# Routing of a gathered token block dealt out differently: three heads sorted early, two pieces a turn

## The chip, the cores and the metric

The kernel runs on one core of a Trainium2 chip. The metric is device microseconds of one execution, lower is better: 1499.62 us is the median of three runs before (1498.49 to 1500.58). An execution with a profile was taken beside them.

## The reference

One encoder block on 512 tokens of 1024 channels: a gated half, an attention half, an output product, and then PEER, a retrieval over 128 x 128 single-neuron experts, which fills most of the time. For each block of 128 tokens PEER does this, 8 heads, 16 experts a head:

```python
q = (xb @ w_query).reshape(128, 8, 2, 128)
s = jnp.einsum('thpc,pkc->thpk', q, sub_keys)
s1, i1 = lax.top_k(s[:, :, 0], 16)
s2, i2 = lax.top_k(s[:, :, 1], 16)
cand = s1[..., :, None] + s2[..., None, :]
sc, ci = lax.top_k(cand.reshape(128, 8, 256), 16)
e = i1[ci // 16] * 128 + i2[ci % 16]
g = softmax(sc)
act = gelu(einsum('td,thkd->thk', xb, expert_u[e]))
out = einsum('thk,thkd->td', g * act, expert_v[e])
```

So each token has 16 lists of 128 scores (8 heads, two halves of the key), each of which is cut to its best 16; then each head chooses 16 among sums of the two lists, and the choices are decoded into expert numbers.

## The kernel before

The four blocks of 128 tokens go two ways. Three blocks are *dense*: all 16384 experts are computed for them, in 128 turns of 128 experts. The fourth block is *gathered*: for each of its tokens the 128 chosen expert rows are fetched by an indirect DMA (8 KB a row, 128 rows a fetch, one for each token), and VectorE does the dot product and the weighted sum.

**Query phase** (250 to 345 us of the trace). For each of 16 columns `c` (head `c // 2`, half `c % 2`), TensorE makes the queries of all four blocks, then the scores of 128 keys; ScalarE copies them to the tile `sc` (two buffers). VectorE sorts the three dense lists of the column with `top16` (maximum of 8, their indices, replace, maximum of 8, indices). The list of the gathered block is put away: `Q.dma_start(sd[:, c, :], sc[:, DB, :])` on line 732, a DMA of 64 KB on SyncE's queue to the tensor `sd` in HBM. TensorE meanwhile runs products of later turns, up to 31 of them (`AHEAD`). When VectorE has finished the dense routing, TensorE turns it (line 815).

**Turns** (from 562 us on, the loop over `e` in 0 to 127). Turn `e` has the same work each time:
- TensorE: 24 matmuls of a u product (line 200: 16 with `uhi`, 8 with `ulo`) of the experts that lie 36 turns ahead, then 18 matmuls of the v product of turn `e` (line 1007). From turn 92 on no u product is left, and only the 18 remain.
- ScalarE: casts `uhi`, `vhi` and `wahi` (lines 169 and 79), and the gelu `act` of the u product (line 759).
- VectorE: `wa` (line 992), `vlo` and `walo` (line 80), `ulo` (line 180): the rests that the casts leave. `uhi`, `ulo`, `vhi`, `vlo` have two buffers each.
- SyncE: the next 512 KB of `uraw`, the next 512 KB of `vraw`, every fourth turn 768 KB of `wt`.

Every engine runs its queue in the order in which the program was written, so a wait of VectorE holds up all that stands behind it.

**Routing of the gathered block.** `gather_routing` is a generator. It loads the 16 lists (`scg`, 1 MB) in turn 0, sorts the two lists of each of 8 heads, chooses for pairs of heads, and decodes four heads at a time (`decode`), with a softmax in between; it stops at each `yield`. In each turn, behind the turn's own VectorE work, three pieces are taken from it (line 1087). There are 26 pieces, so that it ends in turn 8 with the expert list `ei`; then the first four gathers are issued on GpSimd (line 953), and from turn 9 on `rate` dot products are put into each turn, a third of that in turns from 92 on. In a turn with dot products these stand ahead of `ulo` and `vlo` on VectorE. `rate` is 128 over the weighted number of turns left: 128 / (123 - 8 - 23.4) = 1.397 with an end in turn 8. In the tail it is 0.35 times that.

In `decode`, ScalarE's part is the copies into the one-hot tiles `oh` (line 676), between a part of VectorE that makes `rw`, `cl` and a part that compares and sums; the softmax has an exponential on ScalarE (line 700), which needs a load of its function table, and the next gelu another.

Names in the rows of the trace: `gs`, `gi` are the sorted values and indices of the gathered block (`late` in the code), `gtop`, `gci` the chosen ones, `uv` a gathered row.

## Time and profile before

| | |
|---|---|
| median of three runs | 1499.62 us |
| profiled execution | 1503.86 us |
| its span, first to last instruction | 1501.6 us |
| busy: TensorE matmuls, weight loads | 97%, 86% |
| busy: VectorE, ScalarE, GpSimd | 77%, 43%, 19% |
| granted TensorE clock, mean | 0.993 |
| DMA over the span | 359.31 MB, 239 GB/s |

The profiled execution is 4.2 us above the median; differences are taken within it and then set against the median. TensorE is busy nearly all the time, so that a share of the span says little here: what counts is where it stands still, and at which clock it runs right behind such a stop. The turns repeat to the hundredth of a microsecond where nothing disturbs them, so that a disturbed stretch can be measured as the excess over so many undisturbed turns.

### The profile page before, as it was taken

The numbers are of one execution on the slowest core, as the hardware profiler recorded it, in microseconds if no ns is written. First come the engines' busy times: TensorE is split into PE (matmuls) and PEld (weight loads), VectorE is DVE, ScalarE is ACT, GpSimd is POOL, SyncE is SP. The second block draws the span as 40 slices with busy tenths as digits, with TensorE's granted clock in tenths as the row PEclk, the third lists the DMA queues.
The fourth block names the chain that finished last, engine by engine and source line by source line (L and its number), as shares of the span: only waits on it lengthen the run. The fifth ranks groups of instructions, "written<-read, shape, count | busy, mean of one in ns | idle before, by whom it ended". The sixth has DMA issues, their size and how long they took to land.

```text
span 1501.6 us, 21590 instructions
## 1 busy us (share of the span) xinstructions
PE 1459.0 (97%) x7945; PEld 1296.2 (86%) x7945; DVE 1161.3 (77%) x2415; ACT 640.3 (43%) x1088; POOL 281.0 (19%) x222
## 2 busy tenths in 40 slices
PE   8999999998999999899999999999999999999997
PEld 6878988888888899789999999999999999987785
DVE  4745554799999958879888888888888888877765
ACT  5455753344555543343333333333333333324334
POOL 0140002445400000012222212222212221211002
PEclk9999999999999999999999999999999999999999
DMA  6331032332366775389999999899999999988764
GB/s 218 105 101 51 22 127 91 95 95 90 113 255 265 253 274 203 105 308 354 340 338 326 331 328 336 322 327 315 337 335 322 323 321 327 324 284 292 253 199 166
DMA packets 129641, 359.31 MB, mean 239 GB/s; under 512 B 9216, under 2 KB 60672, under 8 KB 113024
## 3 DMA queue, kind: packets, MB, share of 16 engines
q1 hardware_dynamic: 104048, 198.54, 40.3%
q0 software_dynamic: 18432, 134.23, 23.6%
q10 hardware_dynamic: 7056, 25.18, 4.2%
q8 instruction: 62, 1.02, 0.3%
q14 instruction: 43, 0.35, 0.1%
HBM read 327.50 MB, written 30.41 MB: 238 GB/s over the span
## 4 chain that ended last, share of the span: by engine, by line
PE 72%; DVE 13%; DMA 7%; ACT 3%; issue 3%; POOL 1%; ACTq 0%; SPq 0%; DVEq 0%; POOLq 0%
PE pu L200 31%; PE acc L1007 27%; PE acc L251 6%; DMA vraw<-in_uv_dram 4%; DVE ohb L846 3%; DVE ulo L180 2%; DVE oha L850 2%; DVE vlo L80 1%; DMA uraw<-in_uT_dram 1%; ACT vhi L79 1%; PE tr L729 1%; PE tr L433 1%; PE pu L251 1%; POOL ulo L180 1%; PE acc L446 1%
## 5 line engine op out<-in xcount | busy, mean ns | idle before, releaser
L200 PE MATMUL pu<-h2T,uhi 128*128 128x384 f32 (+2 forms) x2336 | 452.4, 343 | 4.9 <-ACT act L759 2.4
L200 PEld LDWEIGHTS pu<-h2T,uhi 128*128 128x128 f32 x2336 | 410.6, 189 | 21.3 <-ACT uhi L169 3.0
L953 POOL DMA_INDIRECT uv<-in_uv_dram,ei x128 | 168.3, 1315 | 844.0 <-DVE xlast L968 352.0
L80 DVE TENSOR_TENSOR vlo<-vraw,vhi 128x1024 fp32r<-128x1024 f32 x128 | 156.8, 1225 | 155.7 <-ACT vhi L79 155.7
L79 ACT CAST vhi<-vraw 128x1024 fp32r<-128x1024 f32 x128 | 134.6, 1051 | 287.2 <-issue 174.7
L200 PE MATMUL pu<-h2T,ulo 128*128 128x384 f32 (+2 forms) x1168 | 236.2, 342 | 7.4 <-DVE ulo L180 5.2
L1007 PE MATMUL acc<-vhi,wahi 128*128 128x512 f32 x768 | 239.4, 392 | 2.2 <-ACT wahi L79 2.2
L1007 PE MATMUL acc<-vlo,wahi 128*128 128x512 f32 x768 | 239.1, 392 | 0.4
L1007 PE MATMUL acc<-vhi,walo 128*128 128x512 f32 x768 | 238.2, 391 | 0.0
L200 PEld LDWEIGHTS pu<-h2T,ulo 128*128 128x128 f32 x1168 | 204.9, 189 | 13.8 <-DVE ulo L180 6.4
L169 ACT CAST uhi<-uraw 128x1024 fp32r<-128x1024 f32 x144 | 150.7, 1047 | 63.1 <-DMA uraw<-in_uT_dram 49.8
L1007 PEld LDWEIGHTS acc<-vlo,wahi 128*128 128x128 f32 x768 | 144.4, 189 | 33.9 <-DVE vlo L80 2.4
L1007 PEld LDWEIGHTS acc<-vhi,walo 128*128 128x128 f32 x768 | 144.2, 188 | 31.6 <-DVE walo L80 0.7
L968 DVE SCALAR_TENSOR_TENSOR xlast<-uv,dot,xlast 128x1024 f32<-128x1024 f32 x128 | 164.5, 1285 | 4.5
L1007 PEld LDWEIGHTS acc<-vhi,wahi 128*128 128x128 f32 x768 | 143.2, 188 | 27.3 <-ACT wahi L79 3.5
L959 DVE SCALAR_TENSOR_TENSOR uv<-uv,h 128x1024 f32<-128x1024 f32 x128 | 153.7, 1219 | 9.5 <-DMA uv<-in_uv_dram,ei 9.5
L180 DVE TENSOR_TENSOR ulo<-uraw,uhi 128x1024 fp32r<-128x1024 f32 x116 | 141.6, 1220 | 22.6 <-ACT uhi L169 22.3
L759 ACT ACTIVATE act<-pu 128x384 f32<-128x384 f32 x128 | 62.9, 491 | 220.6 <-PE pu L200 220.2
L180 POOL TENSOR_TENSOR ulo<-uraw,uhi 128x512 fp32r<-128x512 f32 x56 | 81.3, 1475 | 209.3 <-PE acc L251 106.3
L79 ACT CAST wahi<-wa 128x384 fp32r<-128x384 f32 x128 | 65.3, 510 | 41.2 <-DVE wa L992 41.2
L992 DVE TENSOR_TENSOR wa<-act,wt 128x384 f32<-128x384 f32 x128 | 70.6, 551 | 2.2 <-DMA wt<-wd 2.1
L80 DVE TENSOR_TENSOR walo<-wa,wahi 128x384 fp32r<-128x384 f32 x128 | 70.7, 553 | 0.6 <-ACT wahi L79 0.6
(250 smaller groups left out, 1475.7 us busy)
## 6 DMA issues: line engine op xcount, KB each, us to landing
uraw<-in_uT_dram SPq DMA_DIRECT2D x128, 512.0 KB, 6.1
vraw<-in_uv_dram SPq DMA_DIRECT2D x128, 512.0 KB, 5.6
wd<-wst ACTq DMA_DIRECT2D x48, 512.0 KB, 2.8
wt<-wd SPq DMA_DIRECT2D x32, 768.0 KB, 11.2
wraw<-in_w_in_dram SPq DMA_DIRECT2D x19, 512.0 KB, 3.7
uraw<-in_w_q_dram SPq DMA_DIRECT2D x16, 512.0 KB, 3.8
xT<-in_xT_dram SPq DMA_DIRECT2D x8, 256.0 KB, 3.7
xt<-in_x_dram SPq DMA_DIRECT2D x1, 2048.0 KB
```

The lines of the kernel that those rows point to most:

```text
L79: S.copy(hi, src)
L80: sub.tensor_tensor(lo, src, hi.bitcast(F32), op=ALU.subtract)
L169: S.copy(hi, raws[i])
L180: eng.tensor_tensor(lo[:, k, :], raws[i][:, k, :], hi[:, k, :].bitcast(F32), op=ALU.subtract)
L200: T.matmul(o, l[:, k, :], r[:, k, t0:n], start=(p == 0 and k == 0), stop=(p == 2 and k == KT - 1))
L251: T.matmul(out[b], l[:, b * 128:(b + 1) * 128], r[:, kk, :], start=(k == 0 and i == 0), stop=(k == KT - 1 and i == 2))
L759: S.activation(acts[e], o[:, :DT], AF.Gelu_apprx_tanh)
L953: G.indirect_dma_start(out=uvs[r].rearrange("p s d -> p (s d)"), out_offset=None, in_=A["uv"], in_offset=bass.IndirectOffsetOnAxis(ap=ei[: ...
L959: V.scalar_tensor_tensor(uv[:, 0, :], uv[:, 0, :], 1.0, h2, op0=ALU.mult, op1=ALU.mult, accum_out=d[:, 0:1])
L968: V.scalar_tensor_tensor(xlast, uv[:, 1, :], d[:, 1:2], xlast, op0=ALU.mult, op1=ALU.add)
L992: eng.tensor_tensor(wa.rearrange("p (c t) -> p c t", c=NWC), acts.pop(e).rearrange("p (c t) -> p c t", c=NWC), wts[e // WG][:, :, e % WG, ...
L1007: T.matmul(acc[b][n], l[:, c], r[:, n * 512:(n + 1) * 512], start=(e == 0 and i == 0), stop=(e == NK - 1 and i == 2))
```

## The change

Three edits, all about the gathered block's routing.

1. The lists of heads 0 to 2 (`SOON = 3`) are no longer put away. In the query phase, columns 0 to 5, they are sorted with the three dense lists straight from `sc`, into tiles that now live longer (`late` in a pool `lt` of its own, opened early). Six DMAs of 64 KB go, and the load of `scg` shrinks from 1 MB to 640 KB. The sorts of three heads leave the turns.
2. The pieces are dealt out by the value that the generator yields: two a turn at most, and a turn ends early where it yields `None`.
3. The parts of `decode` and `softmax` are called one by one: ScalarE's copies and its exponential come in the turn after the one in which VectorE made their inputs, and VectorE's comparisons in the turn after that.

The turns are now: 0 the load; 1 sort of head 3 and choice for heads 0, 1; 2 sorts of heads 4 and 5; 3 choice 2, 3 and sort 6; 4 sort 7 and choice 4, 5; 5 choice 6, 7; 6 softmax's subtraction and the first decode's VectorE part; 7 ScalarE alone; 8 the first decode's comparisons and sums, softmax's sums, the second decode's first part; 9 ScalarE alone; 10 the second decode's comparisons and sums, and `ei`. The routing ends in turn 10, and `rate` becomes 128 / (123 - 10 - 23.4) = 1.429.

```diff
@@ query phase
-        Q.dma_start(sd[:, c, :], sc[:, DB, :])
-        top16([(dense[0][:, h, b, p, :], dense[1][:, h, b, p, :], sc[:, b, :]) for b in range(DB)])
+        lists = [(dense[0][:, h, b, p, :], dense[1][:, h, b, p, :], sc[:, b, :]) for b in range(DB)]
+        if h < SOON:
+            lists.append((late[0][:, h, 0, p, :], late[1][:, h, 0, p, :], sc[:, DB, :]))
+        else:
+            Q.dma_start(sd[:, c, :], sc[:, DB, :])
+        top16(lists)
@@ gather_routing
-        Q.dma_start(scg, sd)
+        Q.dma_start(scg[:, 2 * SOON:, :], sd[:, 2 * SOON:, :])
         Q.dma_start(h2, hd)
-        for _ in range(3):
-            yield
-        for h in range(H):
-            top16([(late[0][:, h, 0, p, :], late[1][:, h, 0, p, :], scg[:, 2 * h + p, :]) for p in range(2)])
-            yield
+        yield None
...
-        for h in range(0, H, 2):
-            top16([(gtop[:, g, 0, :], gci[:, g, 0, :], candidates(gp, late, g)[:, 0, :]) for g in (h, h + 1)])
-            yield
+        for h in range(SOON, H):
+            sort(h)
+            yield 1
+            if h % 2:
+                choose(h - 3)
+                yield 1
+        choose(H - 2)
+        yield None
         gating = softmax(gp, gtop, groute[2])
-        for h in range(0, H, 4):
-            next(gating, None)
-            next(gating, None)
-            yield from decode(gp, late[1][:, h:h + 4], gci[:, h:h + 4], [r[:, h:h + 4] for r in groute])
+        next(gating)
+        first, second = decoded(0), decoded(4)
+        next(first)
+        yield None
+        next(first)
+        next(first)
+        next(gating)
+        yield None
+        next(first)
+        yield 1
+        next(first)
+        next(gating)
+        next(second)
+        yield None
+        next(second)
+        next(second)
+        yield None
+        next(second)
+        yield 1
+        next(second)
@@ the loop over e
-            for _ in range(3):
-                if next(routing, True):
-                    routing = None
+            for _ in range(2):
+                if next(routing, 0) != 1:
                     break
-            if routing is None:
+            if routing.gi_frame is None:
+                routing = None
                 refill()
```

Where the instructions stand now. VectorE, a column of the query phase (column 0), before:

```order
L613 MAX s_2176<-sc 128x8 x3
L615 MAX_INDEX i_2177<-s_2176,sc 128x8 x3
L617 MATCH_REPLACE sc<-s_2176,sc 128x128 x3
L619 MAX s_2176<-sc 128x8 x3
L621 MAX_INDEX i_2177<-s_2176,sc 128x8 x3
```

and of the changed kernel (whose line numbers are its own):

```order
L618 MAX s_2179<-sc 128x8 x3
L618 MAX gs_2181<-sc 128x8
L620 MAX_INDEX i_2180<-s_2179,sc 128x8 x3
L620 MAX_INDEX gi_2182<-gs_2181,sc 128x8
L622 MATCH_REPLACE sc<-s_2179,sc 128x128 x3
L622 MATCH_REPLACE sc<-gs_2181,sc 128x128
L624 MAX s_2179<-sc 128x8 x3
L624 MAX gs_2181<-sc 128x8
L626 MAX_INDEX i_2180<-s_2179,sc 128x8 x3
L626 MAX_INDEX gi_2182<-gs_2181,sc 128x8
```

Five instructions a column have come in, for columns 0 to 5; the numbers behind `s`, `i`, `gs`, `gi` are the program's buffer numbers.

VectorE around the first decode, from its last instruction (`fi`) to the comparisons on `oh`, before:

```order
L669 CAST fi<-gi_5710 128x128
L992 TENSOR_TENSOR wa<-act,wt 128x384
L80 TENSOR_TENSOR vlo<-vraw,vhi 128x1024
L80 TENSOR_TENSOR walo<-wa,wahi 128x384
L180 TENSOR_TENSOR ulo<-uraw,uhi 128x1024
L683 TENSOR_TENSOR oh<-oh,iota_b 128x1024 x2
L685 TENSOR_TENSOR oh<-oh,fi 128x1024 x2
```

and of the changed kernel:

```order
L674 CAST fi<-gi_2182 128x128
L1026 TENSOR_TENSOR wa<-act,wt 128x384
L81 TENSOR_TENSOR vlo<-vraw,vhi 128x1024
L81 TENSOR_TENSOR walo<-wa,wahi 128x384
L181 TENSOR_TENSOR ulo<-uraw,uhi 128x1024
L1026 TENSOR_TENSOR wa<-act,wt 128x384
L81 TENSOR_TENSOR vlo<-vraw,vhi 128x1024
L81 TENSOR_TENSOR walo<-wa,wahi 128x384
L181 TENSOR_TENSOR ulo<-uraw,uhi 128x1024
L688 TENSOR_TENSOR oh<-oh,iota_b 128x1024 x2
L690 TENSOR_TENSOR oh<-oh,fi 128x1024 x2
```

A whole turn of plain work now stands between the two; the same holds for the second decode.

ScalarE at the first decode, before:

```order
L79 CAST wahi<-wa 128x384
L700 ACT_TABLE_LOAD
L700 ACTIVATE groute_5707<-groute_5707 128x128
L676 CAST oh<-rw 128x1024
L676 CAST oh<-cl 128x1024
L759 ACT_TABLE_LOAD
L759 ACTIVATE act<-pu 128x384
```

and of the changed kernel:

```order
L768 ACTIVATE act<-pu 128x384
L170 CAST uhi<-uraw 128x1024
L80 CAST vhi<-vraw 128x1024
L80 CAST wahi<-wa 128x384
L681 CAST oh<-rw 128x1024
L681 CAST oh<-cl 128x1024
L705 ACT_TABLE_LOAD
L705 ACTIVATE groute_5736<-groute_5736 128x128
L768 ACT_TABLE_LOAD
L768 ACTIVATE act<-pu 128x384
```

The exponential has moved behind the copies and both stand in the turn after the one whose VectorE work they read. The order on TensorE is the same in both kernels. From the last u product on, ScalarE's order is the same too.

## Rows read from the trace of the kernel before

**Rows 1.** The page's first part: busy time of TensorE's matmuls, its share of the span, and their number.

```profile
PE 1459.0 (97%) x7945; PEld 1296.2 (86%) x7945; DVE 1161.3 (77%) x2415; ACT 640.3 (43%) x1088; POOL 281.0 (19%) x222
```

**Rows 2.** The view of waits, TensorE alone, from 560 to 700 us: who waited for whom, microseconds in total, times, longest.

```profile
PE pu L200 <- DVE ulo L180: 5.2, 3, 2.0
PE pu L200 <- ACT uhi L169: 1.8, 1, 1.8
```

**Rows 3.** The view by windows: the stretch, its length, busy microseconds (and instructions) of TensorE, its weight loads, VectorE, ScalarE and GpSimd, then the granted TensorE clock, the busy share of the DMA engines and their GB/s.

```profile
624.00:630.00 6.00, 5.40 (x22) 5.40 (x23) 4.47 (x6) 4.17 (x6) 0.00 (x0) 0.72 0.34 92
700.00:800.00 100.00, 100.00 (x508) 91.08 (x507) 84.50 (x120) 39.09 (x69) 24.62 (x18) 1.00 0.94 342
1100.00:1200.00 100.00, 100.00 (x508) 91.08 (x507) 82.39 (x118) 36.38 (x65) 23.19 (x17) 1.00 0.92 320
1400.00:1460.00 60.00, 57.73 (x244) 46.32 (x244) 42.75 (x64) 20.95 (x33) 2.02 (x2) 0.97 0.65 208
```

**Rows 4.** The timeline of TensorE from 560 to 700 us: start, length, what ran, and in brackets the idle time before it and what ended it. L200 is the u product of a turn (16 matmuls with `uhi`, then 8 with `ulo`), L1007 the v product; 566.33 is the start of the v product of turn 0, 669.17 that of turn 11 and 677.48 that of turn 12.

```profile
566.33 0.63 PE L1007 MATMUL acc<-vhi,wahi 128*128 128x512 f32 x2
...
612.22 2.96 PE L200 MATMUL pu<-h2T,uhi 128*128 128x384 f32 x16
617.01 1.68 PE L200 MATMUL pu<-h2T,ulo 128*128 128x384 f32 x8 [1.83 <-DVE ulo L180]
...
624.60 4.43 PE L200 MATMUL pu<-h2T,uhi 128*128 128x384 f32 x16 [1.78 <-ACT uhi L169]
...
639.55 2.93 PE L200 MATMUL pu<-h2T,ulo 128*128 128x384 f32 x8 [2.02 <-DVE ulo L180]
...
659.34 1.68 PE L200 MATMUL pu<-h2T,ulo 128*128 128x384 f32 x8 [1.35 <-DVE ulo L180]
...
669.17 0.63 PE L1007 MATMUL acc<-vhi,wahi 128*128 128x512 f32 x2
...
677.48 0.63 PE L1007 MATMUL acc<-vhi,wahi 128*128 128x512 f32 x2
```

**Rows 5.** The timeline of VectorE from 570 to 614 us, in the same columns: where in turns 1 to 4 the pieces of the gathered block begin (`gs<-scg` the first sort of a turn, `cand<-gs` the first choice) and where the next turn begins (`wa<-act,wt`).

```profile
575.71 0.48 DVE L613 MAX8 gs<-scg 128x8 f32<-128x128 f32 x2
...
582.73 0.54 DVE L992 TENSOR_TENSOR wa<-act,wt 128x384 f32<-128x384 f32 x1
...
585.93 0.48 DVE L613 MAX8 gs<-scg 128x8 f32<-128x128 f32 x2
...
600.84 0.87 DVE L637 TENSOR_TENSOR cand<-gs 128x16 f32<-128x16 f32 x10
...
603.24 0.54 DVE L992 TENSOR_TENSOR wa<-act,wt 128x384 f32<-128x384 f32 x1
...
613.68 0.53 DVE L992 TENSOR_TENSOR wa<-act,wt 128x384 f32<-128x384 f32 x1
```

**Rows 6.** The timeline of VectorE from 612 to 660 us: the second half of the routing (`oh` the one-hot work, `ei` the list of experts), two turns' beginnings left out, and the first dot product of a gathered row.

```profile
628.27 1.29 DVE L683 TENSOR_TENSOR oh<-oh,iota_b 128x1024 bf16<-128x1024 bf16 x2
...
630.68 1.60 DVE L690 TENSOR_TENSOR oh<-oh 128x512 bf16<-128x512 bf16 x6
...
636.20 0.55 DVE L992 TENSOR_TENSOR wa<-act,wt 128x384 f32<-128x384 f32 x1
...
645.03 1.55 DVE L690 TENSOR_TENSOR oh<-oh 128x512 bf16<-128x512 bf16 x6
...
647.30 0.23 DVE L946 CAST ei<-groute 128x128 int32<-128x128 f32 x1
...
656.91 1.23 DVE L959 SCALAR_TENSOR_TENSOR uv<-uv,h 128x1024 f32<-128x1024 f32 x1 [8.91 <-DMA uv<-in_uv_dram,ei]
```

**Rows 7.** The timeline of ScalarE from 560 to 700 us: the first cast of the v rows that waits for TensorE alone, and a load of ScalarE's function table.

```profile
579.00 1.05 ACT L79 CAST vhi<-vraw 128x1024 fp32r<-128x1024 f32 x1 [0.58 <-PE acc L1007]
...
621.83 1.28 ACT L759 ACT_TABLE_LOAD   x1
```

**Rows 8.** The timeline of VectorE from 255 to 296 us, where a score column's lists are sorted (steps 1, 2, 3 and 6 of the query; `cand` marks the end of step 1's sorts), and under it, from the view of waits from 250 to 400 us, TensorE's wait for the finished routing.

```profile
261.88 0.68 DVE L613 MAX8 s<-sc 128x8 f32<-128x128 f32 x3 [2.77 <-ACT sc L731]
...
265.41 0.58 DVE L637 TENSOR_TENSOR cand<-s 128x48 f32<-128x48 f32 x5
268.27 0.68 DVE L613 MAX8 s<-sc 128x8 f32<-128x128 f32 x3 [2.28 <-ACT sc L731]
...
274.62 0.68 DVE L613 MAX8 s<-sc 128x8 f32<-128x128 f32 x3 [0.39 <-ACT sc L731]
...
293.66 0.68 DVE L613 MAX8 s<-sc 128x8 f32<-128x128 f32 x3 [2.23 <-ACT sc L731]
...
PE po L815 <- DVE route L692: 1.5, 1, 1.5
```

**Rows 9.** DMA: the gather's queue (packets, MB, share), two issues of the page (count, KB each, us to landing), the GB/s of forty slices from 700 to 760 us, and from the view of the gather's line the least, median and greatest time from issue to landing.

```profile
q0 software_dynamic: 18432, 134.23, 23.6%
...
uraw<-in_uT_dram SPq DMA_DIRECT2D x128, 512.0 KB, 6.1
...
wt<-wd SPq DMA_DIRECT2D x32, 768.0 KB, 11.2
...
GB/s 339 407 284 350 363 358 442 410 183 333 305 304 406 416 396 387 426 413 398 410 374 426 289 178 188 339 208 333 191 273 382 360 390 426 378 311 349 418 431 415
...
DMA to landing us min/median/max: 5.5/8.8/13.2
```

More of the change, by code (lines that the diff above doesn't have):

```diff
@@ L36 @@
 WG = 4
+SOON = 3
 RING = 36
@@ L602, in peer_block @@
     ring = ctx.enter_context(tc.tile_pool(name="ring", bufs=RING))
+    lt = ctx.enter_context(tc.tile_pool(name="lt", bufs=1))
     rt_ctx = ExitStack()
@@ L608, in peer_block @@
     dense = (rt.tile([128, H, DB, 2, TOPK], F32, name="s16"), rt.tile([128, H, DB, 2, TOPK], U32, name="i16"))
+    late = (lt.tile([128, H, 1, 2, TOPK], F32, name="gs16"), lt.tile([128, H, 1, 2, TOPK], U32, name="gi16"))
     def top16(lists):
@@ L920, in peer_block @@
     ei = gp.tile([128, 128], I32, name="ei")
-    late = (gp.tile([128, H, 1, 2, TOPK], F32, name="gs16"), gp.tile([128, H, 1, 2, TOPK], U32, name="gi16"))
     h2 = gp.tile([128, 1024], F32, name="h2")
@@ L926, in gather_routing, with sort, choose, decoded @@
         scg = ex.tile([128, 2 * H, NK], F32, name="scg", tag="uv", bufs=UVB)
-        Q.dma_start(scg, sd)
+        Q.dma_start(scg[:, 2 * SOON:, :], sd[:, 2 * SOON:, :])
         Q.dma_start(h2, hd)
-        for _ in range(3):
-            yield
-        for h in range(H):
-            top16([(late[0][:, h, 0, p, :], late[1][:, h, 0, p, :], scg[:, 2 * h + p, :]) for p in range(2)])
-            yield
+        yield None
         gtop = gp.tile([128, H, 1, TOPK], F32, name="gtop")
         gci = gp.tile([128, H, 1, TOPK], U32, name="gci")
-        for h in range(0, H, 2):
+        def sort(h):
+            top16([(late[0][:, h, 0, p, :], late[1][:, h, 0, p, :], scg[:, 2 * h + p, :]) for p in range(2)])
+        def choose(h):
             top16([(gtop[:, g, 0, :], gci[:, g, 0, :], candidates(gp, late, g)[:, 0, :]) for g in (h, h + 1)])
-            yield
-        gating = softmax(gp, gtop, groute[2])
-        for h in range(0, H, 4):
-            next(gating, None)
-            next(gating, None)
-            yield from decode(gp, late[1][:, h:h + 4], gci[:, h:h + 4], [r[:, h:h + 4] for r in groute])
+        def decoded(h):
+            return decode(gp, late[1][:, h:h + 4], gci[:, h:h + 4], [r[:, h:h + 4] for r in groute])
+        for h in range(SOON, H):
[6 more added lines that the diff above has]
+        yield None
+        gating = softmax(gp, gtop, groute[2])
+        next(gating)
[18 more added lines that the diff above has]
+        next(second)
         fl = lambda t: t.rearrange("p h b k -> p (h b k)")
```

## The prediction

> **What bounds the kernel now.** I read the page first: TensorE's matmuls are busy 1459.0 us, 97% of the span [rows 1], so about 42 us of standing still is all that reordering can win, unless TensorE also runs slowly somewhere. Then the view of waits, stretch by stretch, for TensorE alone. The reader is to see that the stretch in which the gathered block is routed has 7.0 us of waits: three for VectorE's `ulo` (5.2 us) and one for ScalarE's `uhi` (1.8 us) [rows 2]. Behind it, from 700 to 800 us, and in the later hundred shown, TensorE is busy 100.00 of 100 us at full clock [rows 3]: there nothing can be won, and something can be lost.
>
> The timeline gives the price of the routing stretch. An undisturbed turn takes 677.48 − 669.17 = 8.31 us. From the v product of turn 0 to that of turn 11 it is 669.17 − 566.33 = 102.84 us, where eleven turns would take 91.41: **11.4 us too much** [rows 4]. The waits are 7.0 of it. The rest is speed: behind a wait, 16 matmuls that take 2.96 us take 4.43, and eight take 2.93 where eight behind another wait take 1.68 [rows 4]; from 624 to 630 us the granted clock is 0.72, a mixture of the two levels 1.2 and 2.4 GHz [rows 3]. So a microsecond of wait here costs up to 11.4 / 7.0 = 1.6 us.
>
> Why VectorE is late: its plain work of a turn takes 585.93 − 582.73 = 3.20 us, three sorts 582.73 − 575.71 = 7.02 (2.34 each), a choice for two heads 603.24 − 600.84 = 2.40, and three choices with the plain work 613.68 − 603.24 = 10.44 [rows 5]. Turns of 10.2 to 10.4 us do not fit into 8.31. In turns 1 to 4 VectorE falls behind by about 2 us a turn. How far may it? `vlo` of turn e cannot begin before ScalarE's cast `vhi`, which waits for TensorE to end the last turn's v product (at 579.00 it waited for that alone [rows 7]); so VectorE's turn begins at the earliest some 0.8 us after TensorE's, and its `ulo` is done 3.2 us later. It is needed when the 16 `uhi` matmuls of the next turn are over, 8.31 + 2.96 = 11.27 after TensorE's turn began. VectorE may therefore begin a turn up to 11.27 − 3.20 = 8.1 us behind TensorE. In turn 1 it began 2.0 behind (at 575.71 − 3.20, where TensorE's turn 1 began at 566.33 + 4.16, taking half a turn for a v product [rows 4, 5]); four turns of together 3 × 10.22 + 10.44 = 41.1, where 33.2 fit, add 7.9 and give 9.9 in turn 5, 1.8 more than it may. The trace shows a wait of 1.83 there [rows 4]. The model holds, and I use it for the changed order.
>
> **The routing turns of the changed kernel.** Work per turn, from the same rows: turns 1, 3 and 4 have a sort and a choice, 3.20 + 2.34 + 2.40 = 7.94; turn 2 two sorts, 7.88; turn 5 one choice, 5.6. All are under 8.31, so the start of 2.0 behind shrinks to the earliest possible 0.8 by turn 5. Turn 6 has the subtraction and a decode's first part, less than the 636.20 − 630.68 = 5.5 that hold such a part and more [rows 6]; even 8.7 would put the next turn only 0.4 later. Turn 7 has nothing but the plain 3.20. Turn 8 is the long one: 636.20 − 628.27 = 7.93 for comparisons, sums, softmax and the second first part [rows 6], so 11.1 with the plain work. It puts turn 9 at 0.8 + 11.1 − 8.3 = 3.6 behind, under the 8.1 allowed, and turn 9, which is plain, brings it back. Turn 10: 3.20 + (630.68 − 628.27) + (647.30 + 0.23 − 645.03) = 8.1. **No wait of TensorE is left in turns 1 to 11.**
>
> ScalarE's pieces in turn 7 are two one-hot copies of about 1 us, two table loads of 1.28 [rows 7] and a short exponential, near 4.9 us on top of about 2.7 of plain casts and gelu: under 8.31, and its inputs are a turn old, so it waits for nothing. I cost it at nothing; what covers it is that `uhi` is cast a whole turn before its use. If the cover failed, the price is a wait like the 1.78 us one [rows 4], at most 2.8 us with its slow clock.
>
> **What stays.** The first gather. `ei` is done at 647.53, the first dot product begins at 656.91, 9.4 us later [rows 6], and `ulo` stands behind it on VectorE. That is the fourth wait, 1.35 us [rows 4]. The changed order has the same: turn 10 ends at 0.8 + 8.1 − 8.3 = 0.6 after TensorE's turn 11 began; the dot product starts at 10.0, `ulo` ends 2.4 later at 12.4, and is needed at 11.3. Wait 1.1 us. With its clock it costs 1.1 to 1.8; I take 1.4. Landing times of gathers run from 5.5 to 13.2 us around a median of 8.8 [rows 9], so this wait may vanish, or be 4.4 longer: a cost from 0 to 5.8.
>
> **The query phase.** Thirty instructions come in, six lists of (265.41 − 261.88) / 3 = 1.18 us each [rows 8], 7.1 us of VectorE's time. Each step's sorts wait for ScalarE's copy: the idle times ahead of steps 1, 2, 3 and 6 are 2.77, 2.28, 0.39 and 2.23 us, and steps 4 and 5 repeat the pair of 2 and 3 [rows 8]. Lag after each added list: step 0, 1.18 − 2.77, none; step 1, 1.18 − 2.28, none; step 2, 1.18 − 0.39 = 0.8; step 3, 0.8 + 1.18 − 2.2, none; 4 and 5 the same. So all of it lies in idle time, with 0.3 us to spare per pair, and the lag never exceeds one of the two `sc` buffers. Cost 0. Without the cover all 7.1 us arrive where TensorE waits for the finished routing (1.5 us now [rows 8]). The six DMAs that go and the smaller `scg` save nothing: the sorts in turn 1 did not wait for `scg` (no bracket at 575.71 [rows 5]).
>
> **The gather phase.** Gathers start two turns later, and `rate` is 1.429 for 1.397. The totals agree: 83 turns × 1.397 and 81 × 1.429 both leave 115 dot products done at turn 91 and the last 13 in turns 92, 94, ..., 116. So the tail keeps its order, and its 2.3 us of idle time from 1400 to 1460 us [rows 3] stays; I take 0, with 2.3 either way.
>
> **Sum.** −11.4 + 1.4 = −10.0 us. In the profiled execution that is 1503.86 → 1493.9. The median of the runs lies 4.2 us lower; I take the stall to be the same there: **1489.6 us**. Bounds of this case: with no gather wait and an idle-free tail 1499.6 − 11.4 − 2.3 = 1485.9; with the late gather (5.8) 1494.0, and 1496.3 with a worse tail as well.
>
> **Rivals.**
> 1. *Bytes, not TensorE, set the gather stretch; no change.* A gather moves 134.23 MB / 128 = 1.049 MB, `uraw` and `vraw` 0.524 each, `wt` 0.197 a turn [rows 9]: 2.71 MB a turn before, 2.74 after, 326 and 330 GB/s. If the queues were the limit, the gathers, beginning 6.7 us later (`ei` at 566.33 − 4.16 + 11 × 8.31 + 0.6 = 654.2, against 647.5), would lose that and save only the 2.5 MB that two turns have loaded by then, 7.5 us at 330: 1498.8. For it: the DMA engines are 92 to 94% busy. Against: 342 GB/s were carried from 700 to 800 us, and TensorE lost nothing there [rows 3].
> The Trainium skill, page "Perfetto Trace Analysis", section "Identifying the Most-Contended Engine", has a rule that speaks for this rival: judge DMA by the used share of HBM bandwidth, TensorE by its weight loads, and work on the higher one. The page "DMA: Bandwidth & Descriptors", section "Specifications", gives about 358 GB/s a core; 330 is 92% of it, weight loads 91.08 of 100, so by that rule the DMA is level with TensorE and the sum would be this rival's. The trace disagrees with 358 as a ceiling: slices of 1.5 us reach 442 GB/s [rows 9].
> 2. *The query's cover fails.* The 7.1 us come back at line 815: 1496.7. Against it stands the working above; for it, that the spare is only 0.3 us per pair of steps.
> 3. *A wait moves into turns 8 to 12*, by ScalarE's table loads or a late first gather: 4.4 us of the gain go, 1494.
> 4. *Slower: late gathers.* The dot products stand ahead of `ulo`. If the queues can't carry 330 GB/s in the long run, each of the 81 full turns with dot products grows. The gain is gone when a turn takes 10.0 / 81 = 0.12 us more, 8.43 us, that is below 325 GB/s. At the 320 GB/s of the lowest window [rows 3] a turn takes 8.57: 81 × 0.26 − 10.0 = +11, 1511. For it: only the windows that ran at 320. Against: TensorE waited for nothing in them, so 320 was the demand.
>
> **How the numbers follow.** Forecast 0.74, rival 1 0.08, rival 2 0.05, rival 3 0.08, rival 4 0.05. The range goes from 1485.9 to 1496.7: it holds the forecast, rivals 2 and 3, and leaves out 1 and 4. A measurement here can tell about 0.2%, 3.0 us, from no change. Faster: forecast, rival 3 and half of rival 2, 0.85; the same: rival 1 and the other half, 0.10; slower: rival 4, 0.05.
>
> **What would show it.** In the profile after: waits of TensorE from 560 to 700 us of about 1.1 us, one only, on `ulo`, in turn 12; no stretch near 0.7 of the clock; from the v product of turn 0 to that of turn 13 about 13 × 8.31 + 1.4 = 109.4 us. On VectorE, idle times ahead of the first six steps of the query mostly gone, and TensorE's wait at line 815 still near 1.5 us. From then on 100 of 100 us busy. The prediction is wrong if TensorE waits for `ulo` in turns 8 to 11, if the wait at line 815 grows, or if turns with dot products become longer than 8.31.

## The result, and the profile after

The changed kernel takes **1489.47 us** (median of 6 runs, 1486.33 to 1491.0); the kernel before, on the same chip, 1500.06 (6 runs, 1498.19 to 1502.91). The ratio is 0.9928, 95% interval 0.9916 to 0.9941: faster by 0.7%, 0.1 us from the forecast (in part by luck, as the part on the prediction says). The profiled execution took 1490.96 us, its span is 1489.2 us, the mean granted clock 0.996 (before 0.993).

The timeline of TensorE, first v product of turn 0 and of turn 13 (columns as in [rows 4]):

```profile
567.02 0.63 PE L1041 MATMUL acc<-vhi,wahi 128*128 128x512 f32 x2
...
675.01 0.63 PE L1041 MATMUL acc<-vhi,wahi 128*128 128x512 f32 x2
```

675.01 − 567.02 = 107.99 us is 13 turns of 8.307. In the kernel before the same 13 turns took 119.45 (turn 13 at 685.78). So 11.46 us have gone from this stretch. The view of waits, which held 7.0 us there [rows 2], has no line at all from 560 to 720 us. The view by windows (columns as in [rows 3]) shows the same stretch at full clock and without a gap:

```profile
624.00:630.00 6.00, 6.00 (x31) 5.26 (x29) 1.61 (x3) 5.35 (x7) 0.00 (x0) 1.00 0.51 175
656.00:700.00 44.00, 44.00 (x226) 40.28 (x225) 36.42 (x52) 15.74 (x29) 13.43 (x11) 1.00 0.97 366
700.00:800.00 100.00, 100.00 (x507) 91.04 (x506) 84.87 (x121) 37.08 (x66) 23.22 (x17) 1.00 0.94 340
1100.00:1200.00 100.00, 100.00 (x507) 91.00 (x506) 82.49 (x118) 36.78 (x66) 23.52 (x18) 1.00 0.92 329
1400.00:1460.00 60.00, 58.44 (x257) 47.67 (x256) 40.54 (x60) 20.68 (x33) 3.58 (x3) 1.00 0.70 230
```

Read the count as well as the busy time: from 624 to 630 us 31 matmuls for 22, and the clock 1.00 for 0.72. The window from 1100 to 1200 us is as it was; from 1400 to 1460 us TensorE stands idle for 1.6 us where it was 2.3.

The timeline of VectorE where turns 2 to 5 begin, which answers to [rows 5]:

```profile
580.90 0.54 DVE L1026 TENSOR_TENSOR wa<-act,wt 128x384 f32<-128x384 f32 x1
...
588.79 0.53 DVE L1026 TENSOR_TENSOR wa<-act,wt 128x384 f32<-128x384 f32 x1
...
596.73 0.54 DVE L1026 TENSOR_TENSOR wa<-act,wt 128x384 f32<-128x384 f32 x1
...
604.89 0.54 DVE L1026 TENSOR_TENSOR wa<-act,wt 128x384 f32<-128x384 f32 x1
```

A turn of TensorE begins 4.18 us (its 24 u matmuls) ahead of its v product. TensorE's turns 2 to 5 began at 579.45, 587.76, 596.07 and 604.37, so VectorE was 1.4, 1.0, 0.7 and 0.5 us behind: it catches up, where before it fell 2 us further behind in each of these turns.

The timeline of VectorE through the second half of the routing, which answers to [rows 6]: turn 8's pieces, the next turn's `wa`, the finished list `ei`, the first dot product, the `ulo` behind it.

```profile
633.36 1.29 DVE L688 TENSOR_TENSOR oh<-oh,iota_b 128x1024 bf16<-128x1024 bf16 x2
...
641.24 0.55 DVE L1026 TENSOR_TENSOR wa<-act,wt 128x384 f32<-128x384 f32 x1
...
654.96 0.23 DVE L980 CAST ei<-groute 128x128 int32<-128x128 f32 x1
655.11 0.55 DVE L1026 TENSOR_TENSOR wa<-act,wt 128x384 f32<-128x384 f32 x1
661.93 1.23 DVE L993 SCALAR_TENSOR_TENSOR uv<-uv,h 128x1024 f32<-128x1024 f32 x1 [6.27 <-DMA uv<-in_uv_dram,ei]
...
663.08 1.22 DVE L181 TENSOR_TENSOR ulo<-uraw,uhi 128x1024 fp32r<-128x1024 f32 x1
```

TensorE's turn 9 began at 641.78 − 4.18 = 637.60, VectorE's at 641.24: 3.6 behind, as worked out ahead. The list is done at 655.19, and the first dot product starts 6.74 us later, not 9.38 as before: `ulo` ends at 664.30, 1.2 us before TensorE wants it.

ScalarE's part of the first decode, in its timeline, goes from the first copy into `oh` to the next gelu:

```profile
622.59 1.04 ACT L681 CAST oh<-rw 128x1024 bf16<-128x1024 int32 x1
...
627.50 0.49 ACT L768 ACTIVATE act<-pu 128x384 f32<-128x384 f32 x1
```

The query phase, timeline of VectorE (first sorts of steps 1 to 4) and two lines of the view of waits from 250 to 400 us, to be set beside [rows 8]:

```profile
262.31 0.68 DVE L618 MAX8 s<-sc 128x8 f32<-128x128 f32 x3 [1.60 <-ACT sc L736]
...
268.70 0.68 DVE L618 MAX8 s<-sc 128x8 f32<-128x128 f32 x3 [1.12 <-ACT sc L736]
...
275.75 0.67 DVE L618 MAX8 s<-sc 128x8 f32<-128x128 f32 x3
...
281.40 0.68 DVE L618 MAX8 s<-sc 128x8 f32<-128x128 f32 x3 [0.39 <-ACT sc L736]
...
DVE s L618 <- ACT sc L736: 11.8, 7, 6.3
...
PE po L824 <- DVE route L697: 1.5, 1, 1.5
```

VectorE's waits for `sc` were 18.6 us (9 times) before: 6.8 of the 7.1 us of added sorts were taken from idle time, and TensorE's wait for the routing is still 1.5 us.

### The profile page after: what moved, and what is told of

It is laid out like the page before. It is cut to its first block, busy times and chain, and to the rows that moved or that the text cites. A ratio compares the mean times of both kernels' runs of the same rounds, so it can differ in the third digit from the quotient of the medians.

```text
span 1489.2 us, 21574 instructions
## 1 busy us (share of the span) xinstructions
PE 1453.4 (98%) x7945; PEld 1292.6 (87%) x7945; DVE 1159.6 (78%) x2415; ACT 641.3 (43%) x1088; POOL 283.6 (19%) x222
## 4 chain that ended last, share of the span: by engine, by line
PE 78%; DVE 9%; DMA 5%; issue 3%; ACT 3%; POOL 1%; ACTq 0%; SPq 0%; DVEq 0%; POOLq 0%
PE pu L201 34%; PE acc L1041 30%; PE acc L252 6%; DMA vraw<-in_uv_dram 3%; DVE ohb L855 3%; DVE oha L859 2%; DVE ulo L181 1%; DMA uraw<-in_uT_dram 1%; PE tr L734 1%; PE pu L252 1%; PE tr L434 1%; POOL ulo L181 1%; PE acc L447 1%; DVE vlo L81 1%; DMA xt<-in_x_dram 1%
```

## The experiments

"Excess" is the time from the v product of turn 0 to that of turn 13, less 13 × 8.307 us; "start" is when the v product of turn 0 begins; "rest" goes from that of turn 13 to the end of the span. All three come from each run's one trace. The ratio is to the kernel before on the same chip, with its 95% interval.

| kernel | us | ratio | start | excess | rest |
|---|---|---|---|---|---|
| before | 1500.06 | | 566.33 | 11.46 | 815.8 |
| before, a second trace | 1499.13 | | 564.56 | 10.93 | 813.3 |
| changed | 1489.47 | 0.9928 (0.9916–0.9941) | 567.02 | 0.00 | 814.2 |
| e1 no early sorts | 1488.5 | 0.9923 (0.9902–0.9945) | 564.92 | 0.00 | 813.4 |
| e2 ScalarE in the same turn | 1498.63 | 0.9989 (0.998–0.9999) | 564.18 | 10.46 | 814.5 |
| e3 early sorts alone | 1495.36 | 0.996 (0.9945–0.9975) | 564.29 | 7.83 | 813.3 |
| e4 all sorts early | 1499.08 | 0.9996 (0.9984–1.0009) | 574.62 | 0.00 | 812.9 |
| e5 gathers end before the tail | 1484.41 | 0.99 (0.9883–0.9918) | 565.44 | 0.00 | 809.7 |
| e6 two empty turns more | 1487.86 | 0.9925 (0.9906–0.9943) | 563.84 | 0.00 | 814.1 |
| e7 e2, first dot a turn later | 1490.65 | 0.9949 (0.9932–0.9965) | 565.27 | 2.83 | 812.8 |
| e8 three pieces, no early sorts | 1493.15 | 0.9961 (0.9947–0.9975) | 565.52 | 5.18 | 814.5 |
| e9 e1 and e5 together | 1484.07 | 0.9903 (0.9886–0.9919) | 565.26 | 0.00 | 809.4 |
| e10 1.75 dot products a turn | 1490.04 | 0.9951 (0.9933–0.9969) | 565.15 | 0.00 | 809.8 |
| e11 same turn, plain turns kept | 1489.11 | 0.9923 (0.9906–0.9939) | 564.72 | 0.68 | 814.7 |

The two traces of the kernel before differ by 1.8 us at the start and 2.5 in the rest; the excess is the column that repeats.

**e1, no early sorts.** `SOON = 0`; a pair's choice comes behind its second sort, and the routing ends in turn 11.

```diff
-SOON = 3
+SOON = 0
...
-                choose(h - 3)
+                choose(h - 1)
...
-        choose(H - 2)
-        yield None
```

> The changed kernel without its first edit: all eight heads are sorted in the turns, still two pieces a turn and ScalarE's part a turn behind; the routing ends in turn 11. My theory, that TensorE waits only where VectorE begins a turn more than 8.1 us late: every turn stays under 8.31 us of VectorE work (a sort and a choice 7.94, two sorts 7.88), so no wait of TensorE in turns 1 to 11, 1489.5 us, ratio to the kernel before 0.993. Rival, that the early sorts carry the gain because they take work out of the turns: three sorts of 2.34 us are back, 7.0 us, and the waits with them, 1494 to 1500 us, ratio 0.996 to 1.000.

1488.5 us and no excess, as my theory had it. The first edit isn't needed once the other two are there.

**e2, ScalarE's part in the same turn.** The pieces of the changed kernel without the `yield None` around ScalarE's part; ends in turn 8.

```diff
         next(gating)
+        next(gating)
         first, second = decoded(0), decoded(4)
         next(first)
-        yield None
         next(first)
         next(first)
-        next(gating)
         yield None
         next(first)
-        yield 1
         next(first)
         next(gating)
         next(second)
-        yield None
         next(second)
         next(second)
         yield None
         next(second)
-        yield 1
         next(second)
```

> The changed kernel without its third edit: early sorts and two pieces a turn stay, but ScalarE's copies and the exponential stand in the turn whose VectorE work they read; the routing ends in turn 8. My theory: VectorE is never late by more than 8.1 us, but ScalarE now waits for VectorE twice and holds its next casts and the gelu; by the durations of the trace the gelu of turn 7 then ends about 0.5 us after TensorE wants its PSUM tile in turn 9 and the next uhi cast 1.5 us late, so one wait of 1.5 us and a following one of 0.8 us on ulo in turns 8 to 10, 2.3 to 3.7 us in all: 1492 to 1493 us, ratio 0.995. Rival, that this edit does nothing because its work was hidden anyway: 1489.5 us, ratio 0.993. Rival, that it carries most of the gain: 1496 or more, ratio 0.997.

Nearly the whole gain is gone, which is the second rival's range, so I had priced this wrong. Its timeline of TensorE has three waits:

```profile
636.46 3.07 PE L201 MATMUL pu<-h2T,uhi 128*128 128x384 f32 x16 [1.55 <-ACT uhi L170]
640.28 1.67 PE L201 MATMUL pu<-h2T,ulo 128*128 128x384 f32 x8 [0.74 <-DVE ulo L181]
...
654.34 2.93 PE L201 MATMUL pu<-h2T,ulo 128*128 128x384 f32 x8 [5.47 <-DVE ulo L181]
```

and its timeline of VectorE shows how VectorE came to be late:

```profile
622.56 1.22 DVE L81 TENSOR_TENSOR vlo<-vraw,vhi 128x1024 fp32r<-128x1024 f32 x1 [5.04 <-ACT vhi L80]
...
637.39 1.23 DVE L81 TENSOR_TENSOR vlo<-vraw,vhi 128x1024 fp32r<-128x1024 f32 x1 [3.62 <-ACT vhi L80]
...
644.86 0.23 DVE L976 CAST ei<-groute 128x128 int32<-128x128 f32 x1
...
651.91 1.23 DVE L989 SCALAR_TENSOR_TENSOR uv<-uv,h 128x1024 f32<-128x1024 f32 x1 [6.36 <-DMA uv<-in_uv_dram,ei]
```

The two in-order queues wait for each other: ScalarE's copies stand behind VectorE's part, ScalarE's `vhi` behind the copies, VectorE's `vlo` behind `vhi` (5.04 and 3.62 us idle). VectorE finishes the list 7.5 us behind TensorE's turn, and then waits 6.4 us for the first gather, with `ulo` behind it. A stall on `vhi` of this length isn't the loss by itself. In the changed kernel VectorE's timeline has one too, and TensorE waited for nothing:

```profile
630.62 1.23 DVE L81 TENSOR_TENSOR vlo<-vraw,vhi 128x1024 fp32r<-128x1024 f32 x1 [5.01 <-ACT vhi L80]
```

Two causes were left: ScalarE's place in the order, or the lateness with which VectorE meets the gather. e7 and e11 part them.

**e7, e2 with the first dot product a turn later.** The gathers are issued as before.

```diff
                 rate = 128.0 / ((NK - 5 - e) - (1.0 - SLOW) * RING)
+                quota = -0.99
```

> The kernel with ScalarE's part in the same turn (1498.6 us), but the first dot product a turn later than there; the gathers are still issued when the list of experts is ready. My theory: that kernel lost its time mostly because VectorE met the first gather 7.4 us behind TensorE, so that the 6.4 us of waiting for the gather went straight on to ulo (a wait of TensorE of 5.5 us and a stretch at the lower clock behind it). A turn of plain work in between takes VectorE back, and the gather has landed by then: no wait of 5.5 us, only the two before it of 1.55 and 0.74 us stay; 10.4 us of excess from turn 0 to 13 fall to about 3, and the time to 1490 to 1492.5. Rival: it is ScalarE's part in the same turn by itself that costs, wherever the first dot product stands: 1495.5 to 1499.

1490.65 us, in the range of my theory. Two waits are left in its timeline of TensorE:

```profile
637.55 3.05 PE L201 MATMUL pu<-h2T,uhi 128*128 128x384 f32 x16 [1.55 <-ACT uhi L170]
641.36 1.66 PE L201 MATMUL pu<-h2T,ulo 128*128 128x384 f32 x8 [0.76 <-DVE ulo L181]
```

The excess falls from 10.46 to 2.83, to what these two cost. So 7.6 us of e2's loss were the late meeting with the gather.

**e11, ScalarE in the same turn, VectorE's order kept.** Against the changed kernel only ScalarE's instructions move; the turn of plain work between the parts stays.

```diff
         next(gating)
+        next(gating)
         first, second = decoded(0), decoded(4)
         next(first)
+        next(first)
+        next(first)
         yield None
-        next(first)
-        next(first)
-        next(gating)
         yield None
         next(first)
         yield 1
         next(first)
         next(gating)
         next(second)
+        next(second)
+        next(second)
         yield None
-        next(second)
-        next(second)
         yield None
```

> The changed kernel with ScalarE's copies and its exponential back in the turn whose VectorE work they read, but with VectorE's order kept, so that a turn of plain work stays behind each part of a decode (ends in turn 10). My theory: what wins is that VectorE has a plain turn in which it comes back, so that it meets the first gather about 1 us behind TensorE; where ScalarE's instructions stand counts for less: no wait of TensorE over 1 us from 560 to 720 us, 1488.5 to 1491. Rival: it is the place of ScalarE's instructions (its casts queue behind copies that wait for the end of VectorE's part), and the waits for uhi and ulo come back: 1494 to 1498.5.

1489.11 us, as the changed kernel. Its timelines, of VectorE first and then of TensorE, show the same stalls on `vhi` as e2:

```profile
623.10 1.23 DVE L81 TENSOR_TENSOR vlo<-vraw,vhi 128x1024 fp32r<-128x1024 f32 x1 [5.04 <-ACT vhi L80]
...
643.14 1.23 DVE L81 TENSOR_TENSOR vlo<-vraw,vhi 128x1024 fp32r<-128x1024 f32 x1 [3.63 <-ACT vhi L80]
...
653.86 0.23 DVE L980 CAST ei<-groute 128x128 int32<-128x128 f32 x1
...
661.14 1.23 DVE L993 SCALAR_TENSOR_TENSOR uv<-uv,h 128x1024 f32<-128x1024 f32 x1 [6.58 <-DMA uv<-in_uv_dram,ei]
...
663.57 1.68 PE L201 MATMUL pu<-h2T,ulo 128*128 128x384 f32 x8 [0.39 <-DVE ulo L181]
```

and they cost 0.4 us of wait in all, because a plain turn follows each. What pays in the third edit is the plain turn that it puts behind each part, not that ScalarE runs later.

**e3, early sorts alone.** The first edit on the kernel before, whose `gather_routing` and loop (three pieces a turn) stay; the sorts begin at head 3.

```diff
-        for h in range(H):
+        for h in range(SOON, H):
             top16([(late[0][:, h, 0, p, :], late[1][:, h, 0, p, :], scg[:, 2 * h + p, :]) for p in range(2)])
```

> The first edit alone on the kernel before: heads 0 to 2 are sorted with the queries, the other nine sorts and choices are still dealt out three a turn and decode runs as before. My theory: turns 1 to 3 have 10.2, 10.3 and 10.4 us of VectorE work, VectorE is 8.0 us late at turn 4, just within the 8.1 allowed, so the first wait (1.83 us) goes; then ScalarE's waits for VectorE come on top of that lag and the waits on uhi and ulo return, together 4 to 6 us with the slow clock: 1494 to 1497 us, ratio 0.996 to 0.998. Rival, that the early sorts carry the gain: 1489.5 us, ratio 0.993.

1495.36 us, in the range of my theory. The first wait for `ulo` is gone; four waits of together 5.0 us are left, two for `uhi` and two for `ulo`.

**e8, three pieces a turn, no early sorts.** e1 with the loop's old number.

```diff
-            for _ in range(2):
+            for _ in range(3):
                 if next(routing, 0) != 1:
```

> The third edit without the first and without its two pieces a turn: all eight heads sorted in the turns, three pieces a turn, ScalarE's part a turn behind; ends in turn 9. My rule of 8.1 us: turns 1 to 4 hold 10.3 us of VectorE's work each, which puts it 2.0 + 4 x 2.0 = 9.9 behind in turn 5, so TensorE waits for ulo there, once or twice, about 1.8 us in all, and nowhere else, since the turns behind it are short; with its clock 2 to 4 us over the kernel without early sorts (1488.5): 1490.5 to 1492.5. Rival: ScalarE's delay alone is enough, 1489 or less. Second rival: without two pieces a turn nothing is won, 1496 or more.

Its timeline of TensorE:

```profile
616.13 1.66 PE L201 MATMUL pu<-h2T,ulo 128*128 128x384 f32 x8 [1.68 <-DVE ulo L181]
...
660.57 1.67 PE L201 MATMUL pu<-h2T,ulo 128*128 128x384 f32 x8 [2.26 <-DVE ulo L181]
```

The first wait is the one I worked out (1.8). The second I missed: VectorE, 4.2 us behind when the list is done, meets the first gather too late. That put the 1493.15 us above my range. No run has the second edit alone: what two pieces a turn are worth, 4.7 us, is read with the third edit in place (e8 less e1).

**The first gather, in the kernels that waited for it and two that didn't.** The rule that allows VectorE 8.1 us, written for this place: `ulo` ends 2.37 us after the dot product starts (661.93 to 664.30 in the changed kernel) and is wanted 11.27 us after the turn began (a turn's begin is again its v product less 4.18 us). So the wait is the list's lateness, plus the time from the list to the dot product, plus 2.37, less 11.27:

| kernel | list done behind the turn's begin | list to first dot | by the rule | in the trace |
|---|---|---|---|---|
| e1 | 0.69 | 6.89 | −1.3 | none |
| changed | 0.98 | 6.74 | −1.2 | none |
| e11 | 2.18 | 7.05 | 0.3 | 0.39 |
| e3 | 2.43 | 6.96 | 0.5 | 0.55 |
| before, second trace | 0.79 | 8.85 | 0.7 | 0.80 |
| before | 0.80 | 9.38 | 1.3 | 1.35 |
| e8 | 4.15 | 6.95 | 2.2 | 2.26 |
| e2 | 7.49 | 6.82 | 5.4 | 5.47 |

Lateness and the time to the dot product are taken from the traces, so the table checks the sum and is no forecast. By it the other five kernels whose first dot product stands right behind the list come out at −0.8 to −1.3; none of them waited.

**e12, the kernel before once more**, without any edit, for that 9.38.

> The kernel before, unchanged, for a second trace of its first gather, which began 9.4 us after the list of experts was done, where the other kernels that waited for it took 6.7 to 7.4. Theory: it lies behind the load of wt (768 KB), issued 2.9 us ahead of it on SyncE's queue in this order of work alone; the second trace shows 9 to 10 us again and a wait for ulo of 1 to 2 us. Rival: a gather's landing scatters by some microseconds from run to run: 6.7 to 7.4, and the third wait for ulo is gone, with a time 1 to 2.5 us lower.

8.85 us, with a wait of 0.80: nearer to the theory than to the rival, and a little under both of its ranges. In both traces of before a load of `wt` was issued 2.9 us ahead of the first gather; in every other kernel it came 5.4 us or more ahead, or behind it. That this load makes the gather late would fit, but no run moved it alone: it stays open.

**e4, all sorts early.** `SOON = 8`; no list is put away, `scg` is not loaded, and a choice is all that is left of a turn.

```diff
-SOON = 3
+SOON = 8
...
-            Q.dma_start(sd[:, c, :], sc[:, DB, :])
+            pass
...
-        scg = ex.tile([128, 2 * H, NK], F32, name="scg", tag="uv", bufs=UVB)
-        Q.dma_start(scg[:, 2 * SOON:, :], sd[:, 2 * SOON:, :])
...
-        for h in range(SOON, H):
-            sort(h)
+        for h in range(0, H, 2):
+            choose(h)
             yield 1
```

> The changed kernel with all eight heads sorted in the query phase (the list of the gathered block is never put away, none of it is loaded back). My theory: the six early lists were free because VectorE stood idle there; from the seventh step on only 0.39 + 0.38 + 1.58 us of idle time are left for ten lists of 1.18 us, so 7.6 to 9.4 us arrive at TensorE's wait for the finished routing (now 1.53 us): 1497 to 1499 us, ratio 0.998 to 1.000. Rival, that sorts in the query phase are hidden by TensorE's products whatever their number: 1489.5 us, ratio 0.993.

1499.08 us. The stretch has no excess, and turn 0 begins 574.62 us into the span, some 9.5 us later than elsewhere. The timeline of TensorE shows the cover of the query phase at an end:

```profile
348.01 2.00 PE L733 MATMUL tr<-keys,qT 128*128 128x128 f32 x8 [4.56 <-ACT sc L735]
...
365.09 4.61 PE L200 MATMUL pu<-h2T,uhi 128*128 128x384 f32 x16 [2.87 <-ACT act L767]
...
383.39 1.65 PE L200 MATMUL pu<-h2T,ulo 128*128 128x384 f32 x4 [4.67 <-POOL ulo L180]
```

In the changed kernel the first of these waits isn't there, and the other two are 2.4 and 2.3 us. The place is another than I expected: TensorE's wait for the finished routing is gone, and the time is lost ahead of it. Three heads fit into VectorE's idle time there, eight don't: what is saved in the turns is paid in the query phase.

**e6, two empty turns more** ahead of the second decode's last part; the routing ends in turn 12 and `rate` is 1.461.

```diff
         next(second)
         next(second)
         yield None
+        yield None
+        yield None
         next(second)
```

> The changed kernel with two empty turns put ahead of the last pieces, so that the routing ends in turn 12 and the first gathers are issued right behind a load of 768 KB of wt, as they were in the kernel before (the trace of the changed kernel has its wt load elsewhere and its first gather took 6.7 us from ei to the dot product, not 9.4). My theory, that the first gather was late because of that load: 9 to 10 us from ei to the first dot product and one wait of TensorE for ulo of 0.8 to 1.4 us, 1 to 2 us in all, 1490.5 to 1491.5 us, ratio 0.994. Rival, that the first gather's time was chance: 6 to 7 us again, no wait, 1489.5 us. A later end costs nothing by either.

1487.86 us, no excess. My theory failed and the rival held: the first dot product began 6.94 us after the list was done, and TensorE waited for nothing. The load of `wt` was issued 5.4 us ahead of the first gather here, against 2.9 in the kernel before, so the test is not as close as I meant it. Beginning the gathers two turns later still costs nothing: no sign of rival 1 or 4.

**e5, gathers that end before the last u product**, 1.58 dot products a turn for 1.43.

```diff
-                rate = 128.0 / ((NK - 5 - e) - (1.0 - SLOW) * RING)
+                rate = 128.0 / (NK - RING - 1 - e) + 1e-6
```

> The changed kernel with a rate of 128 / 81 = 1.58 dot products a turn from turn 11 on, so that all 128 gathers are done by turn 91 and none is left for the tail. It raises the bytes of a turn from 2.74 to 2.90 MB, 349 GB/s, and VectorE's work of a turn to about 7.3 of 8.31 us. My theory, that TensorE and not the DMA sets the turns: turns stay at 8.31 us with no wait of TensorE, and the tail, which has neither gathers nor dot products then, loses some of its 1.9 us of waits for wahi: 1486 to 1489.5 us, ratio 0.990 to 0.993. Rival, that the queues carry about 330 GB/s in the long run and set the stretch: a turn takes 2.90 / 0.330 = 8.8 us, 81 times 0.5 = 39 us more, 1528 us, ratio 1.02; if the limit is 342 GB/s, 8.48 us, 14 us more, 1503 us, ratio 1.002.

The best so far, 1484.41 us, below the range of my theory, which had counted the tail's 1.9 us of waits alone. From the view by windows, two stretches of the tail of the changed kernel:

```profile
1350.00:1370.00 20.00, 19.89 (x88) 15.77 (x87) 16.62 (x24) 8.45 (x14) 2.02 (x2) 1.00 0.87 290
1410.00:1430.00 20.00, 18.44 (x81) 14.52 (x80) 16.74 (x25) 8.01 (x13) 0.00 (x0) 1.00 0.52 160
```

and of e5, with the gather phase above:

```profile
700.00:800.00 100.00, 100.00 (x507) 91.04 (x506) 91.00 (x131) 38.20 (x69) 28.02 (x20) 1.00 0.99 368
1350.00:1370.00 20.00, 20.00 (x90) 16.58 (x89) 10.81 (x15) 7.32 (x10) 0.00 (x0) 1.00 0.57 178
1410.00:1430.00 20.00, 20.00 (x90) 16.56 (x89) 10.41 (x16) 7.32 (x10) 0.00 (x0) 1.00 0.61 178
```

In the changed kernel's tail 20 us hold 81 to 88 matmuls where 90 fit, though the busy share reads 92 to 99%; with the gathers over, 90 each time, and the rest of the span is 4.5 us shorter (814.2 to 809.7). In the gather phase the DMA carries 368 GB/s, and TensorE waits for nothing.

**e9, e1 and e5 together.** The edits of e1, and this rate:

```diff
-                rate = 128.0 / ((NK - 5 - e) - (1.0 - SLOW) * RING)
+                rate = 128.0 / (NK - RING - 1 - e) + 1e-6
```

> No early sorts (ends in turn 11), and all dot products before the last u product, so 1.60 a turn. What the two had apart: -1.0 and -5.1 us against the changed kernel. My theory: the routing turns are free of waits with or without the early sorts, and the tail is free of waits at any rate that ends before it, so the kernel is equal to the one with early sorts and this rate: 1483 to 1485.5. Rival: what the early sorts cost in the query phase is real, and the two gains add: 1482.5 to 1483.5.

1484.07 us, the same as e5: the early sorts neither cost nor win, so the two theories' ranges here were too close to part.

**e10, 1.75 dot products a turn.**

```diff
-                rate = 128.0 / ((NK - 5 - e) - (1.0 - SLOW) * RING)
+                rate = 1.75
```

> The changed kernel with 1.75 dot products a turn, so that they end some 7 turns before the last u product. A turn then asks for 1.75 x 1.049 + 1.245 = 3.08 MB, 371 GB/s at 8.31 us. Theory A, bytes are still not what sets a turn (368 GB/s were carried from 700 to 800 us with 1.58 a turn and no wait of TensorE): 1483.5 to 1485.5, as with 1.58. Theory B, about 366 GB/s is the most that the queues carry: turns of 3.08 MB take 8.42 us, 73 of them 8 us more, with waits of VectorE for gathers handed on to ulo: 1489 to 1494.

The median, 1490.04 us, is in theory B's range, and the runs lie far apart, 1484.69 to 1494.55 us (5 runs). The trace is of the shortest of them, and has neither waits nor excess; windows of it:

```profile
700.00:800.00 100.00, 100.00 (x507) 91.04 (x506) 93.28 (x137) 39.11 (x72) 32.10 (x21) 1.00 1.01 377
1000.00:1200.00 200.00, 200.00 (x1013) 182.05 (x1012) 183.67 (x268) 76.53 (x138) 63.87 (x42) 1.00 1.00 373
```

The DMA engines' busy share is 1.00 to 1.01 at 373 to 377 GB/s. The view of waits, VectorE from 700 to 1300 us, one line of e10:

```profile
DVE uv L993 <- DMA uv<-in_uv_dram,ei: 38.8, 26, 2.6
```

for 0.4 us in the changed kernel and 9.3 in e5; and VectorE's waits for `vhi`, which are its spare time, are 92.2 us in the changed kernel, 49.7 in e5 and 9.3 here. So this rate seems to stand on the edge. Whether bytes or VectorE's time give way first in the longer runs isn't seen, since the one trace is of the shortest.

## Why the prediction was right

- **The excess (−11.4).** It counted to turn 11; taken two undisturbed turns on, to turn 13, it is 11.46 us. All of it went, and the second trace of before has 10.93. Of the profiled difference of 12.4 us in the span, −1.6 lies in the rest and +0.7 at the start, both within what two traces of one kernel differ by.
- **VectorE may be 8.1 us behind.** Held where VectorE's own work made it late: turn 9 began 3.6 behind as worked out, without a wait; the first wait of e8 was 1.7 us for 1.8; and the same sum, with the measured lateness put in, gives the six waits of the table above within 0.1 us. It does not foresee a wait for ScalarE's `uhi` (e2, e3).
- **ScalarE's part at nothing.** Right in size, for its instructions: from `oh` at 622.59 to `act` at 627.50 us they took the 4.9 us worked out, and e11 shows that their place hardly matters. The plain turns, which I had only counted as short turns, carry the third edit: without them (e2) all but 0.1% is lost. My expectation for e2, a stall of ScalarE's size, missed this: lateness adds up and is paid at the first gather.
- **The first gather (1.4, from 0 to 5.8).** The one term that was mis-sized: it cost 0. I took the 9.38 us of [rows 6] over; it was 6.74, and 6.8 to 7.4 in the ten kernels of the experiments whose first dot product stands right behind the list. With this term at 0 the sum would have been 1488.2 us; the interval of the ratio, some 9 to 13 us of gain, holds both. The sign that the prediction named, one wait of about 1.1 us in turn 12 and 109.4 us to turn 13, did not come: there is none, and it is 107.99. That the forecast of 1489.6 us and the measured 1489.47 agree to 0.1 us is therefore in part luck: the runs of the changed kernel alone spread over 4.7 us.
- **The query phase at 0.** Confirmed by the idle times, and by e4 from the other side. Against e1 the first edit wins nothing: with two pieces a turn and plain turns the sorts fit without it.
- **The tail at 0.** No change that two traces could tell; the order stayed. The forecast didn't see that this tail was worth some 4.5 us (the rest is 812.8 to 815.8 us in the traces with gathers in the tail, 809.4 to 809.8 in the three without). The idle time shows half of it: in the changed kernel TensorE is busy 153.15 us from 1323.1 to 1478.6, idle 2.35, and in e5 the same work takes 151.0 us. The rest is matmuls that run long behind short waits: a pair took 0.73 us for 0.62 behind the wait of 1.45 us at 1412.59.
- **The rivals.** 1 and 4 (bytes): e5 carried 351 to 368 GB/s from 700 to 1300 us with no wait of TensorE, where rival 4 set its threshold at 325; that an edge lies near 373 is suggested by e10's scatter, but no trace shows it. By the Trainium skill, page "Perfetto Trace Analysis", section "Identifying the Most-Contended Engine", the engine to work on first is the one with the highest occupancy, where the DMA is judged by its used share of HBM bandwidth and TensorE by its weight loads. By an estimate from the 358 GB/s a core that the Trainium skill's page "DMA: Bandwidth & Descriptors", section "Specifications", gives, that was the DMA in e5, at 103% (368 GB/s from 700 to 800 us) against 91% for the weight loads. The traces disagree: in those 100 us TensorE waited for nothing, and its turns stayed at 8.31 us. What e5 won lies in the tail. 2: no wait has grown. 3: no wait in turns 8 to 12; it comes back where VectorE is later when the list is done: 0.4 us in e11, 0.6 in e3, 2.3 in e8, 5.5 in e2.

## What to carry to other kernels

When an engine with an in-order queue may run late, work out by how much, and count every turn's work against that; an occasional empty turn that lets it come back is cheap (e6: two more cost nothing), and a long wait, as for a first gather, should meet the engine when it is early. Moving work ahead of the crowded stretch helps only as far as idle time there covers it (three heads, not eight), and may not be needed if the stretch is dealt out evenly. In a stretch with short waits count matmuls per window, since the idle time showed only half of the loss here.

## What was not expected of the hardware

A wait of TensorE cost 1.2 to 1.7 times its length (excess over waits: 11.46 / 7.0 before, 10.46 / 7.8 in e2, 2.83 / 2.3 in e7, 5.18 / 3.9 in e8, 0.68 / 0.4 in e11), with no fixed price: behind a wait of 2.02 us eight matmuls took 2.93 us [rows 4], behind one of 2.26 us 1.67 (e8). And the DMA engines could be kept at a busy share of 1.00, at 373 GB/s over 200 us, with TensorE busy 200.00 of 200 us beside them; there the time of a run scattered over 10 us.
